# The last sums of a two-block forward pass cut as 384 and 128 tokens, their chunks turned one by one, and the last tile written in two parts

## The chip, the cores and the metric

One core of one Trainium2 chip runs the whole program in one launch. The metric is the device time in microseconds (us). The engines are named as in the profile: PE is TensorE's matmuls, PEld its weight loads, DVE is VectorE, ACT is ScalarE, POOL is GpSimd, and SP is SyncE, which here only issues transfers.

## The reference, cut to what matters

Two transformer blocks follow each other on 16 meta tokens and 512 tokens of width 1024. The part that matters is the very end of the second block: the down projection of its second feed-forward network, the residual sum, and the final norm.

```python
def swiglu_2(x, w_gate, w_up, w_down):
    return (jax.nn.silu(x @ w_gate) * (x @ w_up)) @ w_down      # D_FF = 2816

...
        h = h + 0.5 * swiglu_2(rms_norm(h, ffn2_norm[l]), ...)
    return rms_norm(h, final_norm)                              # out: (1, 512, 1024) f32
```

`rms_norm` divides each token's 1024 values by the root of their mean square and multiplies by a gain for each of the 1024 columns.

## The kernel before

**Layout.** The running sum `h` lies with its 1024 columns over the partitions: eight chunks `h[:, c]` of 128 columns, each with the tokens along the free axis (16 meta tokens, which the output leaves out, then 512). A matmul has 128 x 128 weights and a slice of tokens as its moving operand. Every product is made of three matmuls, since weights and inputs are split into a high and a low part in fp32r: high weights with high input, high weights with low input, low weights with high input (`mm`, L488). Each of the three loads its own weights.

**Weights.** A transfer brings a piece of a weight matrix to one of two raw buffers, ACT casts its high part (`whi`, L120) and DVE subtracts to get the low part (`wlo`, L125). A raw buffer is loaded anew when both have read it.

**The feed-forward network** goes through its 22 chunks of hidden columns in three parts (`PARTS`: 6, 8 and 8). Each part ends with a down projection of what it has, `dn`. In the third part eight chunks of hidden columns (`gh`, `gl`) meet weights for eight output chunks: 24 matmuls for each output chunk and slice of tokens. Four transfers of 1 MB (`in_ffn_w_down`) bring these weights, two output chunks each. `seven` makes the hidden chunks (accumulators `sa`, `sb`, `sc`, L700) and begins the first three `dn` sums with seven of the eight hidden chunks, before the eighth is done: the first sum before the last two products of the eighth (`up_a`, `gate_b`), two more behind them. `up_a` writes the eighth hidden chunk for tokens 16 to 271, `gate_b` for tokens 272 to 527. `finish` adds the eighth.

**The last loop** is where the change lies. It takes the tokens in two halves, `XA = (16, 256)` and `XB = (272, 256)` (start and length), and in each half the eight output chunks `c`:

- PE adds the 24 products in a PSUM bank `dn` (the first three chunks of the first half are those that `seven` began).
- DVE adds the bank to `h` (L1782). ACT squares the sum (L415; L412 for a half's first chunk, L408 for the last half's last), and DVE adds the square to `sqacc` (L416).
- DVE multiplies the sum by the final gain of its columns (`g`, L1786). Two chunks share one tile `g` of 2 x 256.
- After every second chunk `turn_out` is put on a list, and it is run when the next chunk's products have been written: four transposes on PE (`oT<-cst,g`, L1747) turn two chunks for two blocks of 128 tokens, and ACT copies them to the output tiles `o` (L1749), where tokens lie over the partitions.

When a half is summed, `compact` sums the squares over the partitions with matmuls of two columns (`p<-ones,sqacc` and, for the last chunk's square, `p<-ones,sq`, L423) and makes the factor of each token by three Newton steps on DVE (L384 to L391, `nw_v`, `nw_y`). `write` multiplies each tile of 128 tokens by it and sends it out: the first tile of the half by DVE (L1760) and SP's queue, the second by ACT (L1757) and ACT's queue. For the first half this stands behind chunk 1 of the second half; for the second half it is the end of the program.

The order of instructions on each engine is set by a scheduler when the program is built; each engine then works strictly in that order.

Of the kernel before, what the change touches and what calls it, by code (L numbers as in the profile page):

```python
# [8 lines left out]
F32 = mybir.dt.float32  # L9
F32R = mybir.dt.float32r  # L10
I32 = mybir.dt.int32
ACTF = mybir.ActivationFunctionType
ALU = mybir.AluOpType
AX = mybir.AxisListType

P = 128
DM = 1024
KD = 8
DFF = 2816
NM = 16  # L20
# [7 lines left out]
V_F1, V_MIX, V_F2, V_FIN = 48, 56, 64, 72  # L28
# [13 lines left out]

A_SL, B_SL = (0, 272), (272, 256)
XA, XB, XF = (16, 256), (272, 256), (16, 512)


def grid(ap, a):
    return ap.rearrange("p (a b) -> p a b", a=a)
# [175 lines left out]
def two_blocks(ctx: ExitStack, tc, d, out):  # L224
    nc = tc.nc
    pe, act, dve, pool = nc.tensor, nc.scalar, nc.vector, nc.gpsimd

    def open_pool(name, bufs=1, **kw):
        cm = tc.tile_pool(name=name, bufs=bufs, reuse_waits="tile", **kw)
        return cm, cm.__enter__()  # L230

    def close_pool(cm):
        cm.__exit__(None, None, None)
# [9 lines left out]
    def ps(name="ps"):  # L243
        return psp.tile([P, 512], F32, tag="ps", name=name)

    cst = const.tile([P, C_END], F32, name="cst")
    ident = cst[:, C_ID:C_ID + P]
# [8 lines left out]
    accF = hold.tile([P, SEQ], F32, name="accF")  # L256

    def col(i):
        return vec[:, i:i + 1]

    def cut(t, k, sl):
        return t[:, k, sl[0]:sl[0] + sl[1]]
# [131 lines left out]
    sq = {}  # L394

    class Rms:
# [7 lines left out]
        def add(self, src, last=False):  # L404
            n = self.sl[1]
            if self.lone or last:
                t = sq["pool"].tile([P, 272], F32, tag="sqFalse", bufs=sq["bufs"], name="sq")[:, 0:n]
                act.activation(out=t, in_=src, func=ACTF.Square)  # L408
                self.wait.append(t)
            elif self.acc is None:  # L410
                self.acc = accF if n == 512 else sq["pool"].tile([P, 272], F32, tag="sqacc", bufs=2, name="sqacc")[:, 0:n]
                act.activation(out=self.acc, in_=src, func=ACTF.Square)  # L412
            else:
                t = sq["pool"].tile([P, 272 if n <= 272 else 512], F32, tag=f"sq{n > 272}", bufs=sq["bufs"], name="sq")[:, 0:n]
                act.activation(out=t, in_=src, func=ACTF.Square)  # L415
                dve.tensor_tensor(out=self.acc, in0=self.acc, in1=t, op=ALU.add)  # L416
# [65 lines left out]
    def mm(acc, u, kcs, hl, last=None):  # L482

        last = kcs[-1] if last is None else last
        for k in kcs:
            for j, (w, x) in enumerate(((u.hi, hl[0]), (u.hi, hl[1]), (u.lo, hl[0]))):
                for p, sl in acc:
                    pe.matmul(p, lhsT=w[:, k], rhs=cut(x, k, sl), start=(k == 0 and j == 0),  # L488
                              stop=(k == last and j == 2))
# [53 lines left out]
    def run_ffn(ffn, items, slices, down, halves, gcol, xn, spare, last, close_w2=False):  # L543


        cm = None
        if spare is None:
            cm, tp = open_pool("right", side="right")
            W.beside = [tp.tile([P, 512], F32, name=f"rawx{i}") for i in range(2)]
            slots = [Slot(None, *[tp.tile([P, 4 * halves[0][1]], F32R, name=f"x{x}{i}") for x in "hl"])  # L550
                     for i in range(2)]
            w_half, n_half = [(w2, 2)], 2
        else:
            W.beside = [spare[1].tile([P, 512], F32, name=f"rawx{i}") for i in range(2)]
            slots = []
            w_half, n_half = [(w4, 1)], 2
        run_item(items[0], slices)
        slots += [W.reserved.pop(0) for _ in range(3 - len(slots))]
        steps, rest = ffn.prepare(halves, gcol, xn, slots)
        todo, did = items[1:], 0  # L560
        for i, it in enumerate(todo):
            upto = len(steps) * (i + 1) // len(todo)
            run_item(it, slices, steps=steps[did:upto])
            did = upto
        for pool, k in w_half:
            W.reserve(pool, k)
        rest()
        down(0, ())
        for _ in range(n_half):
            W.halve(W.reserved.pop(0))  # L570
        for part in (1, 2):
            first = ffn.seven(range(PARTS[part][1]), slices if part == 1 else last)
            if part == 1:
                down(1, first)
        W.whole(not close_w2)
        own = [x for x in slots if x.pool is not None]
        W.idle.extend(own)
        if cm:
            close_pool(cm)
        return first  # L580
# [374 lines left out]
    p = ps("vt")  # L955
    pe.transpose(p[:, 0:48], gains, ident[0:48, 0:48])
    dve.tensor_copy(out=vec[:, 0:48], in_=p[:, 0:48])
    p = ps("mtT")
# [12 lines left out]
    p = ps("vt")  # L971
    pe.transpose(p[:, 0:P], vrow, ident)
    dve.tensor_copy(out=vec[:, 48:P], in_=p[:, 48:P])
    for i in (1, 5):
        g = vec[:, V_GN[i]:V_GN[i] + KD]
# [12 lines left out]
    i = 0  # L988
    while i < len(order):
        kind, n = order[i]  # L990
# [330 lines left out]
    def add_h(after=None):  # L1321
        def sink(c, sl, p):
            dve.tensor_tensor(out=cut(h, c, sl), in0=p, in1=cut(h, c, sl), op=ALU.add)
            if after:
                after(c)
        return sink
# [389 lines left out]
    for c in ALLK:  # L1716
# [7 lines left out]
    cm_o, op_ = open_pool("outp")  # L1724
    cm_x, wx = open_pool("wx")
# [5 lines left out]
    ob = op_.tile([P, 4, DM], F32, name="o")  # L1731
    sq.update(pool=op_, bufs=2)
    first = run_ffn(ffn, items[2:], ONE, lambda part, first: ffn.down(PARTS[part][1], ONE, add_h(), first), [XA, XB], V_F2,
                    ob.rearrange("p a b -> p (a b)").rearrange("p (k t) -> p k t", k=KD), (wx, op_), [XA])


    halves = [XA, XB]
    fins = {sl: Rms(sl) for sl in halves}
    ot = [ob[:, i] for i in range(4)]

    def turn_out(c, sl, g):

        t0 = (sl[0] - NM) // P
        q = ps("oT")
        for t in range(2):
            for i in range(2):
                pe.transpose(q[:, (2 * t + i) * P:(2 * t + i + 1) * P], g[:, i, t * P:(t + 1) * P], ident)  # L1747
        for t in range(2):
            act.copy(out=ot[t0 + t][:, P * (c - 1):P * (c + 1)], in_=q[:, 2 * t * P:2 * (t + 1) * P])  # L1749

    def write(sl):
        r = fins[sl].r
        t0 = (sl[0] - NM) // P
        for t in range(2):
            o = ot[t0 + t]
            if t:
                act.activation(out=o, in_=o, func=ACTF.Copy, scale=r[:, t:t + 1])  # L1757
                nc.scalar.dma_start(out=out[0, P * (t0 + t):P * (t0 + t + 1)], in_=o)
            else:
                dve.tensor_scalar(out=o, in0=o, scalar1=r[:, t:t + 1], scalar2=None, op0=ALU.mult)  # L1760
                nc.sync.dma_start(out=out[0, P * (t0 + t):P * (t0 + t + 1)], in_=o)

    us, wait = [], []
    ks = list(range(PARTS[2][1]))
    for sl in halves:
        for c in range(KD):
            if first:
                u, (p,) = first.pop(0)
                us.append(u)
                ffn.finish(len(ks), [sl], u, [p])  # L1770
            else:
                if sl == XA:
                    us += W.take(1)
                p = ps("dn")[:, 0:256]
                mm([(p, sl)], us[c], ks, (ffn.gh, ffn.gl))
            if wait:
                wait.pop()()
            if sl == XB and c == 1:
                fins[XA].compact()
                write(XA)  # L1780
            src = cut(h, c, sl)
            dve.tensor_tensor(out=src, in0=p, in1=src, op=ALU.add)  # L1782
            fins[sl].add(src, last=sl == XB and c == KD - 1)
            if c % 2 == 0:
                g = op_.tile([P, 2, 256], F32, tag="g", bufs=2, name="g")
            dve.tensor_scalar(out=g[:, c % 2], in0=src, scalar1=col(V_FIN + c), scalar2=None, op0=ALU.mult)  # L1786
            if c % 2:
                wait.append(lambda c=c, sl=sl, g=g: turn_out(c, sl, g))
    wait.pop()()
    fins[XB].compact()  # L1790
    write(XB)
    close_pool(cm_x)
    close_pool(cm_o)
    ffn.close()
# [44 lines left out]
```

## Time and profile before

| | us |
|---|---|
| median of 3 runs | 2034.89 (2034.45 to 2038.19) |
| profiled execution, its own time | 2036.98 |
| its span, first to last instruction | 2035.2 |
| PE busy | 1995.0 (98%) |
| DVE busy | 1486.4 (73%) |
| ACT busy | 1063.4 (52%) |
| mean granted TensorE clock | 0.994 |

The profiled execution's own time is 1.8 us more than its span, and 2.1 us more than the median. The trace's times count from the first instruction of the span. A matmul's row gives its start and a modelled length; matmuls overlap, so the pace of PE is read from the distance between starts.

### The profile page before, as it was taken

How to read it: one execution, taken by the hardware profiler on the slowest of the kernel's cores; microseconds unless marked ns; L12 is line 12 of the kernel's file. 1: busy time of each engine (PE TensorE's matmuls, PEld its weight loads, DVE VectorE, ACT ScalarE, POOL GpSimd, SP SyncE). 2: the span in 40 equal slices, each digit the busy share in tenths (PEclk: the TensorE clock that was granted, in tenths of full speed). 3: DMA queues.
4: the chain of work that ended last, by engine and by line, in shares of the span. 5: the costliest groups of instructions: out<-in, count | busy, mean ns of one | idle time of the engine just before them, and what ended most of it. 6: DMA issues, size and time to landing. Idle time of an engine off the chain costs nothing.

```text
span 2035.2 us, 34893 instructions
## 1 busy us (share of the span) xinstructions
PE 1995.0 (98%) x13583; PEld 1833.5 (90%) x13583; DVE 1486.4 (73%) x2949; ACT 1063.4 (52%) x2030; POOL 283.2 (14%) x290
## 2 busy tenths in 40 slices
PE   8999999999999999999999999999999999999998
PEld 8999999989989989899998998987777788898998
DVE  5948578777776767668777775876889868685784
ACT  5445345357765445445443543656878743353552
POOL 0012021023420002111000211103211100120210
PEclk9999999999999999999999999999999999999999
DMA  6357575237784238566532766737545353475761
GB/s 182 93 116 166 131 149 147 84 81 174 149 147 125 73 93 166 146 139 157 151 78 78 162 149 140 156 116 159 102 98 114 76 152 99 108 162 140 147 163 44
DMA packets 413212, 260.10 MB, mean 128 GB/s; under 512 B 17483, under 2 KB 405830, under 8 KB 413046
## 3 DMA queue, kind: packets, MB, share of 16 engines
q1 hardware_dynamic: 317446, 192.94, 32.1%
q0 software_dynamic: 95040, 63.69, 22.1%
q8 instruction: 106, 1.74, 0.3%
q10 hardware_dynamic: 560, 1.24, 0.2%
q14 instruction: 60, 0.49, 0.1%
HBM read 230.53 MB, written 4.23 MB: 115 GB/s over the span
## 4 chain that ended last, share of the span: by engine, by line
PE 84%; DVE 8%; ACT 4%; DMA 2%; issue 1%; POOL 0%; ACTq 0%; POOLq 0%; DVEq 0%; SPq 0%
PE dn L488 25%; PE sa L700 18%; PE acc L488 14%; PE sc L700 8%; PE sb L700 4%; PE accB L488 3%; PE accA L488 3%; PE wo L488 2%; DVE wlo L125 1%; ACT whi L120 1%; PE ro L1611 1%; PE p L423 1%; PE num L1202 1%; PE ms L1469 1%; DMA raw<-in_w_uq 1%
## 5 line engine op out<-in xcount | busy, mean ns | idle before, releaser
L120 ACT CAST whi<-raw 128x1024 fp32r<-128x1024 f32 (+3 forms) x500 | 397.5, 801 | 346.3 <-PE dn L488 168.5
L125 DVE TENSOR_TENSOR wlo<-raw,whi 128x512 fp32r<-128x512 f32 (+2 forms) x456 | 406.2, 905 | 134.7 <-ACT whi L120 130.6
L488 PE MATMUL dn<-gh,whi 128*128 128x256 f32 (+2 forms) x908 | 277.5, 326 | 0.6 <-ACT gh L469 0.6
L488 PE MATMUL dn<-gl,whi 128*128 128x256 f32 (+2 forms) x908 | 277.9, 326 | 0.0
L488 PE MATMUL dn<-gh,wlo 128*128 128x256 f32 (+2 forms) x908 | 277.0, 325 | 0.0
L488 PE MATMUL acc<-nh,whi 128*128 128x512 f32 (+2 forms) x600 | 191.0, 353 | 1.1 <-DVE y L1219 1.1
L488 PE MATMUL acc<-nl,whi 128*128 128x512 f32 (+2 forms) x600 | 188.5, 349 | 0.0
L488 PE MATMUL acc<-nh,wlo 128*128 128x512 f32 (+2 forms) x600 | 188.1, 348 | 0.0
L488 PEld LDWEIGHTS dn<-gh,whi 128*128 128x128 f32 x908 | 163.0, 188 | 16.5 <-ACT gh L469 0.8
L488 PEld LDWEIGHTS dn<-gl,whi 128*128 128x128 f32 x908 | 163.1, 188 | 15.5 <-DVE gl L470 0.3
L488 PEld LDWEIGHTS dn<-gh,wlo 128*128 128x128 f32 x908 | 163.2, 188 | 14.8
L700 PE MATMUL sc<-nh,whi 128*128 128x256 f32 (+1 forms) x488 | 137.4, 282 | 0.0
L700 PE MATMUL sa<-nh,whi 128*128 128x256 f32 (+1 forms) x488 | 137.3, 281 | 0.0
L700 PE MATMUL sa<-nh,wlo 128*128 128x256 f32 (+1 forms) x488 | 137.2, 281 | 0.0
L700 PE MATMUL sc<-nh,wlo 128*128 128x256 f32 (+1 forms) x488 | 137.2, 281 | 0.0
L700 PE MATMUL sc<-nl,whi 128*128 128x256 f32 (+1 forms) x488 | 137.1, 281 | 0.0
L700 PE MATMUL sa<-nl,whi 128*128 128x256 f32 (+1 forms) x488 | 137.0, 281 | 0.0
L488 PEld LDWEIGHTS acc<-nh,whi 128*128 128x128 f32 (+1 forms) x600 | 104.6, 188 | 16.4 <-DVE y L1219 1.6
L488 PEld LDWEIGHTS acc<-nh,wlo 128*128 128x128 f32 (+1 forms) x600 | 104.0, 188 | 15.0
L488 PEld LDWEIGHTS acc<-nl,whi 128*128 128x128 f32 (+1 forms) x600 | 103.9, 188 | 13.6
L95 POOL DMA_DIRECT2D raw<-in_ffn_w_up x32 | 41.1, 1284 | 448.8 <-DMA raw<-in_ffn_w_up 229.1
L95 POOL DMA_DIRECT2D raw<-in_ffn_w_in x32 | 41.1, 1283 | 439.4 <-DMA raw<-in_ffn_w_in 163.6
(494 smaller groups left out, 5583.1 us busy)
## 6 DMA issues: line engine op xcount, KB each, us to landing
raw<-in_ffn_w_in SPq DMA_DIRECT2D x56, 512.0 KB, 4.1
raw<-in_ffn_w_gate SPq DMA_DIRECT2D x44, 512.0 KB, 3.6
raw<-in_ffn_w_in SPq DMA_DIRECT2D x64, 256.0 KB, 3.2
raw<-in_ffn_w_out SPq DMA_DIRECT2D x16, 1024.0 KB, 8.0
wlo<-raw POOLq DMA_DIRECT2D x32, 512.0 KB, 5.3
raw<-in_ffn_w_up SPq DMA_DIRECT2D x64, 256.0 KB, 3.2
raw<-in_ffn_w_down SPq DMA_DIRECT2D x16, 1024.0 KB, 7.4
raw<-in_a_w_in SPq DMA_DIRECT2D x18, 512.0 KB, 3.6
```

Source lines behind the costliest of these rows:

```text
L95: self.nc.gpsimd.dma_start(out=dst(t), in_=src, accum_op=ALU.add)
L120: nc.scalar.copy(out=ho, in_=src)
L125: self.lo_engine.tensor_tensor(out=lw, in0=src, in1=ho.bitcast(F32), op=ALU.subtract)
L423: pe.matmul(self.p1[:, self.n:self.n + 2], lhsT=src[:, o:o + P], rhs=ones[:, 0:2], start=True, stop=True)
L488: pe.matmul(p, lhsT=w[:, k], rhs=cut(x, k, sl), start=(k == 0 and j == 0), stop=(k == last and j == 2))
L700: pe.matmul(acc, lhsT=w[:, 4 * i + k], rhs=x[:, k], start=start and k == 0 and j == 0, stop=k == 3 and j == 2, skip_group_check=not start)
L1202: pe.matmul(num[:, c0:SEQ], lhsT=w[0:kk, j], rhs=x[s_], start=(j == 0 and i == 0), stop=(j == 4 and i == 2))
L1469: pe.matmul(s, lhsT=mq[i][a][:, t0:t0 + P], rhs=mk[i][b], start=j == 0, stop=j == 2)
L1611: pe.matmul(o[i], lhsT=vt_[:, i, j], rhs=s_[i, j][b], start=(j == 0 and b == 0), stop=(j == 3 and b == 1))
```

## The change

The two slices of tokens of the last loop become `FA = (16, 384)` and `FB = (400, 128)`: three blocks of 128 tokens, then one. Each chunk has a tile `g` of its own and is turned by itself, so a `turn_out` has three transposes in the first slice and one in the second, and one ACT copy. The sum of squares of the long slice lies in `accF`, and its squares after the first chunk are made and added in two pieces of 192. `write` goes over three tiles (DVE, ACT, DVE) for the first slice, and for the last tile over two pieces of 512 columns: the first by DVE and SP's queue, the second by ACT and ACT's queue.

```diff
+FA, FB = (16, 384), (400, 128)
...
-                self.acc = accF if n == 512 else sq["pool"].tile([P, 272], F32, tag="sqacc", bufs=2, name="sqacc")[:, 0:n]
+                self.acc = accF[:, 0:n] if n > 272 else sq["pool"].tile([P, 272], F32, tag="sqacc", bufs=2, name="sqacc")[:, 0:n]
                 act.activation(out=self.acc, in_=src, func=ACTF.Square)
+            elif 272 < n < 512:
+                for c in (slice(0, n // 2), slice(n // 2, n)):
+                    t = sq["pool"].tile([P, 272], F32, tag="sqFalse", bufs=sq["bufs"], name="sq")[:, 0:n // 2]
+                    act.activation(out=t, in_=src[:, c], func=ACTF.Square)
+                    dve.tensor_tensor(out=self.acc[:, c], in0=self.acc[:, c], in1=t, op=ALU.add)
...
-                    ob.rearrange("p a b -> p (a b)").rearrange("p (k t) -> p k t", k=KD), (wx, op_), [XA])
+                    ob.rearrange("p a b -> p (a b)").rearrange("p (k t) -> p k t", k=KD), (wx, op_), [FA])
...
-    halves = [XA, XB]
+    halves = [FA, FB]
...
-        t0 = (sl[0] - NM) // P
-        q = ps("oT")
-        for t in range(2):
-            for i in range(2):
-                pe.transpose(q[:, (2 * t + i) * P:(2 * t + i + 1) * P], g[:, i, t * P:(t + 1) * P], ident)
-        for t in range(2):
-            act.copy(out=ot[t0 + t][:, P * (c - 1):P * (c + 1)], in_=q[:, 2 * t * P:2 * (t + 1) * P])
+        t0, n = (sl[0] - NM) // P, sl[1] // P
+        q = ps("oT")[:, 0:sl[1]]
+        for t in range(n):
+            pe.transpose(q[:, t * P:(t + 1) * P], g[:, t * P:(t + 1) * P], ident)
+        act.copy(out=ob[:, t0:t0 + n, P * c:P * (c + 1)], in_=grid(q, n))
...
-        for t in range(2):
+        for t in range(sl[1] // P):
             o = ot[t0 + t]
...
+            row = out[0, P * (t0 + t):P * (t0 + t + 1)]
+            for i in range(2 if sl == FB else 1):
+                c = slice(512 * i, 512 * i + 512) if sl == FB else slice(0, DM)
+                if (t + i) % 2 == 0:
+                    dve.tensor_scalar(out=o[:, c], in0=o[:, c], scalar1=r[:, t:t + 1], scalar2=None, op0=ALU.mult)
+                    nc.sync.dma_start(out=row[:, c], in_=o[:, c])
+                else:
+                    act.activation(out=o[:, c], in_=o[:, c], func=ACTF.Copy, scale=r[:, t:t + 1])
+                    nc.scalar.dma_start(out=row[:, c], in_=o[:, c])
...
-            if c % 2 == 0:
-                g = op_.tile([P, 2, 256], F32, tag="g", bufs=2, name="g")
-            dve.tensor_scalar(out=g[:, c % 2], in0=src, scalar1=col(V_FIN + c), scalar2=None, op0=ALU.mult)
-            if c % 2:
-                wait.append(lambda c=c, sl=sl, g=g: turn_out(c, sl, g))
+            g = op_.tile([P, 384], F32, tag="g", bufs=2, name="g")[:, 0:sl[1]]
+            dve.tensor_scalar(out=g, in0=src, scalar1=col(V_FIN + c), scalar2=None, op0=ALU.mult)
+            wait.append(lambda c=c, sl=sl, g=g: turn_out(c, sl, g))
```

In the changed file the lines below the edit stand 6 or 7 further down (L1782 is L1789, L488 is L494). All engines keep their order up to the first `dn` of the last part on PE, and up to the last weights on DVE and ACT.

The first place is DVE's queue where the last loop begins. `wlo_...` are the low parts of the last down projection's weights; `raw_86` holds the fourth and last transfer in the rows of `wlo_17930` and `wlo_17932`, which before stand further down. Before the change the queue reads:

```order
L125 TENSOR_TENSOR wlo_17928<-raw_85,whi_17927 128x1024
L724 SCALAR_TENSOR_TENSOR sqFalse<-sqacc,sqFalse 128x256
L1782 TENSOR_TENSOR h<-dn,h 128x256
L470 TENSOR_TENSOR gl<-sqFalse,gh 128x256
L1786 TENSOR_SCALAR g<-h,vec 128x256
L1782 TENSOR_TENSOR h<-dn,h 128x256 x2
```

The same place of DVE's queue in the changed kernel reads:

```order
L730 SCALAR_TENSOR_TENSOR sqFalse<-sqacc,sqFalse 128x256
L476 TENSOR_TENSOR gl<-sqFalse,gh 128x256
L126 TENSOR_TENSOR wlo_17930<-raw_86,whi_17929 128x1024
L126 TENSOR_TENSOR wlo_17932<-raw_86,whi_17931 128x1024
L1789 TENSOR_TENSOR h<-dn,h 128x384 x2
L1792 TENSOR_SCALAR g<-h,vec 128x384 x2
```

The first sums `h` stood ahead of the last weights' low parts and now stand behind both of them; ACT's two casts `whi_17929` and `whi_17931` likewise stand ahead of the first square now.

The second place is the end of PE's queue: the last `dn` matmuls, the last transposes, and the sums of squares. Before the change it reads:

```order
L488 MATMUL dn<-gh,whi_17931 128x256
L488 MATMUL dn<-gl,whi_17931 128x256
L488 MATMUL dn<-gh,wlo_17932 128x256
L1747 MATMUL oT<-cst,g 128x128
L423 MATMUL p_21529<-ones,sqacc 128x2 x2
L1747 MATMUL oT<-cst,g 128x128 x3
L423 MATMUL p_21529<-ones,sq 128x2 x2
```

The end of PE's queue in the changed kernel reads:

```order
L494 MATMUL dn<-gh,whi_17931 128x128
L494 MATMUL dn<-gl,whi_17931 128x128
L494 MATMUL dn<-gh,wlo_17932 128x128
L1752 MATMUL oT<-cst,g 128x128 x2
L429 MATMUL p_21568<-ones,sqacc 128x2
L429 MATMUL p_21568<-ones,sq 128x2
```

The matmuls are as many as before, 24 for each chunk, with 128 columns for 256; behind the last of them two transposes stand instead of four, and two sums of squares instead of four.

## Rows read from the trace of the kernel before

**Rows 1.** Page, part 1: busy time of each engine.
```profile
PE 1995.0 (98%) x13583; PEld 1833.5 (90%) x13583; DVE 1486.4 (73%) x2949; ACT 1063.4 (52%) x2030; POOL 283.2 (14%) x290
```

**Rows 2.** Chain that ended last, from 1984 us on (start, length, what).
```profile
1991.22 0.44 PE oT L1747 x4
1991.65 5.68 PE dn L488 x48
...
2006.68 0.34 PE p L423 x4
...
2025.41 0.44 DVE h L1782
...
2027.21 0.17 DVE nw_v L439
...
2029.39 1.15 ACT o L1757
```

**Rows 3.** PE's timeline: first and last `dn` of the last part, its wait.
```profile
1972.79 0.28 PE L488 MATMUL dn<-gh,whiwide 128*128 128x256 f32 x1
...
1984.88 0.33 PE L1747 MATMUL oT<-cst,g 128*128 128x128 f32 x1 [0.60 <-DVE g L1786]
...
2025.10 0.28 PE L488 MATMUL dn<-gh,wlo 128*128 128x256 f32 x1
2025.22 0.27 PE L1747 MATMUL oT<-cst,g 128*128 128x128 f32 x1
```

**Rows 4.** PE's timeline: runs of 400 columns and of 144, first and last.
```profile
471.76 0.35 PE L1202 MATMUL num<-sl,vh 128*128 128x400 f32 x1
...
472.31 0.34 PE L1205 MATMUL den<-sl,onesr 128*128 128x400 f32 x1
...
479.38 0.27 PE L1202 MATMUL num<-sl,vh 128*128 128x144 f32 x1
...
479.72 0.27 PE L1205 MATMUL den<-sl,onesr 128*128 128x144 f32 x1
```

**Rows 5.** Timelines of SP, ACT and DVE where the last loop begins.
```profile
1980.32 0.37 SPq L99 DMA_DIRECT2D raw<-in_ffn_w_down  x1
...
1983.70 0.41 ACT L469 CAST gh<-sqFalse 128x256 fp32r<-128x256 f32 x1 [1.85 <-DVE sqFalse L724]
...
1985.58 1.03 ACT L120 CAST whi<-raw 128x1024 fp32r<-128x1024 f32 x1
...
1984.14 0.42 DVE L470 TENSOR_TENSOR gl<-sqFalse,gh 128x256 fp32r<-128x256 f32 x1
...
1984.75 0.74 DVE L1782 TENSOR_TENSOR h<-dn,h 128x256 f32<-128x256 f32 x2
...
1986.64 1.23 DVE L125 TENSOR_TENSOR wlo<-raw,whi 128x1024 fp32r<-128x1024 f32 x1 [0.25 <-ACT whi L120]
```

**Rows 6.** Page, part 6: transfers of these weights, median us from issue to landing.
```profile
raw<-in_ffn_w_down SPq DMA_DIRECT2D x16, 1024.0 KB, 7.4
```

**Rows 7.** Groups by line and shape on DVE: busy us, mean ns.
```profile
L1782 DVE TENSOR_TENSOR h<-dn,h 128x256 f32<-128x256 f32 x16 | 6.7, 423 | 15.7 <-PE dn L488 15.7
L1786 DVE TENSOR_SCALAR g<-h,vec 128x256 f32<-128x256 f32 x16 | 5.6, 352 | 0.4
L1760 DVE TENSOR_SCALAR o<-o,nw_y 128x1024 f32<-128x1024 f32 x2 | 1.5, 755 | 0.1
L454 DVE TENSOR_SCALAR dg<-cst,nw_y 128x128 f32<-128x128 f32 x44 | 10.7, 293 | 4.3 <-PE p L455 3.7
L1481 DVE TENSOR_SCALAR mp<-mp,su 128x512 f32<-128x512 f32 x16 | 7.7, 483 | 0.3
```

**Rows 8.** End of the program: last issues, and transfers in 40 slices from 2030 to 2036 us.
```profile
2030.18 0.36 SPq L1761 DMA_DIRECT2D out<-o  x1
...
2030.57 0.37 ACTq L1758 DMA_DIRECT2D out<-o  x1
...
GB/s 0 0 0 0 0 0 55 382 410 437 410 410 437 410 410 355 410 437 382 437 355 355 437 410 55 0 0 55 0 0 0 0 0 0 0 0 0 0 0 0
```

**Rows 9.** Windows, by engine busy us (x instructions), then granted clock, DMA.
```profile
411.20:414.60 3.40, 3.06 (x29) 2.77 (x28) 1.91 (x10) 2.08 (x6) 0.00 (x0) 1.00 0.00 0
414.60:421.40 6.80, 6.78 (x32) 6.73 (x33) 4.73 (x19) 1.61 (x3) 0.00 (x0) 0.50 0.11 25
670.00:676.40 6.40, 6.40 (x58) 6.34 (x57) 2.08 (x13) 2.50 (x6) 0.00 (x0) 1.00 0.01 3
```

More of the change, by code (lines that the diff above doesn't have):

```diff
@@ L1753, in write @@
         t0 = (sl[0] - NM) // P
-        for t in range(2):
+        for t in range(sl[1] // P):
             o = ot[t0 + t]
[L1756 to L1761, printed above, removed]
+            row = out[0, P * (t0 + t):P * (t0 + t + 1)]
[7 more added lines that the diff above has]
+                    nc.scalar.dma_start(out=row[:, c], in_=o[:, c])
     us, wait = [], []
@@ L1771, in two_blocks @@
             else:
-                if sl == XA:
+                if sl == FA:
                     us += W.take(1)
-                p = ps("dn")[:, 0:256]
+                p = ps("dn")[:, 0:sl[1]]
                 mm([(p, sl)], us[c], ks, (ffn.gh, ffn.gl))
@@ L1777, in two_blocks @@
                 wait.pop()()
-            if sl == XB and c == 1:
-                fins[XA].compact()
-                write(XA)
+            if sl == FB and c == 1:
+                fins[FA].compact()
+                write(FA)
             src = cut(h, c, sl)
             dve.tensor_tensor(out=src, in0=p, in1=src, op=ALU.add)
-            fins[sl].add(src, last=sl == XB and c == KD - 1)
-            if c % 2 == 0:
-                g = op_.tile([P, 2, 256], F32, tag="g", bufs=2, name="g")
-            dve.tensor_scalar(out=g[:, c % 2], in0=src, scalar1=col(V_FIN + c), scalar2=None, op0=ALU.mult)
-            if c % 2:
-                wait.append(lambda c=c, sl=sl, g=g: turn_out(c, sl, g))
+            fins[sl].add(src, last=sl == FB and c == KD - 1)
+            g = op_.tile([P, 384], F32, tag="g", bufs=2, name="g")[:, 0:sl[1]]
+            dve.tensor_scalar(out=g, in0=src, scalar1=col(V_FIN + c), scalar2=None, op0=ALU.mult)
+            wait.append(lambda c=c, sl=sl, g=g: turn_out(c, sl, g))
     wait.pop()()
-    fins[XB].compact()
-    write(XB)
+    fins[FB].compact()
+    write(FB)
     close_pool(cm_x)
```

## Prediction

> **What bounds the kernel now.** I read the page's busy times first: PE is busy for 1995.0 of 2035.2 us [rows 1], so what lengthens PE's stream lengthens the kernel, unless the end gets shorter. The chain that ended last agrees for the part that changes: from 1984 us to 2025 us it is `dn` matmuls and transposes on PE, in runs such as 48 `dn` in 5.68 us and four `oT` in 0.44 us, and only behind the last `dn` does it leave PE, for DVE, ACT and the last transfers [rows 2]. PE's timeline shows one wait there, 0.60 us for a `g` from DVE at 1984.88 us [rows 3]. So the change has three places: PE's stream from the first `dn` at 1972.79 us to the last one at 2025.10 us, the wait at its head, and the tail behind 2025.38 us, where the last `dn` ends (start and length of its row) [rows 3].
>
> **PE's stream.** The last part has 8 x 24 = 192 matmuls for each of the two slices, before and after. What changes is their width, so I need the pace of 384 and of 128 columns. At 256 the chain has 48 in 5.68 us, which is 0.118 us each [rows 2]. Wider: between the first and the last row of the run of 400 columns lie three steps in 0.55 us, 0.183 each [rows 4]. On the line through 256 and 400 (0.00045 us a column) 384 columns take 0.176. Narrower: in the run of 144 columns three steps take 0.34 us, 0.113 each [rows 4]; four transposes of 128 columns take 0.44, 0.110 each, and four sums of two columns stand in the chain with 0.34 [rows 2]. So below some 245 columns a matmul with weights of its own gets no faster: its pace is that of loading 128 x 128 weights. The 128-token slice will pay about 0.112 for each matmul, hardly less than 0.118 for twice the tokens.
>
> The sum: before 384 x 0.118 = 45.3 us. After 192 x 0.176 = 33.8 and 192 x 0.112 = 21.5, together 55.3. That is +10.0 us. Bounds: the narrow pace from 0.110 to 0.118 gives -0.4 to +1.2 around it, the wide one 0.172 to 0.179 gives -0.8 to +0.6.
>
> The row shows 0.113 at 144 columns [rows 4]. The Trainium skill's page "TensorE: Matmul & The Clock Gate", in its section on the back-to-back issue gap, puts the steady pace of pairs of a weight load and a 128-column matmul at about 81 ns. By that the narrow slice would take 192 x 0.081 = 15.6 us, an estimate from that page, the stream would grow by 4.1 and not by 10.0, and the whole sum below would end near 2037.7. The trace does not agree with it for these 4-byte operands, so I go by the row.
>
> Transposes: 28 of the 32 stood ahead of the last `dn`'s end or beside it, now 30 do. At 0.11 each that is +0.2. The first slice's factors need three sums of two columns for four, -0.1. More interruptions with fewer transposes in each cost nothing by themselves, since each pays by its weight loads. The 16 + 8 squares in pieces, the gains and the copies lie on ACT and DVE beside PE: before, DVE waited 15.7 us for PE in front of the 16 `h` [rows 7], and in the long slice a chunk now gives it 4.2 us of PE's time for about 1.8 us of its own work. If that cover were gone, banks would fill and PE would wait for `h`; nothing points to it. The two tiles that DVE now scales for the first slice (2 x 0.755 [rows 7]) stand ahead of the third narrow chunk's `h` and `g`; PE has two chunks of 2.7 us to do meanwhile, some 5 us, against about 4.5 for Newton's steps and the two tiles. That is hidden with little to spare.
>
> **The wait at the head.** PE will come to the first transpose later: from 1972.79, 21 x 0.176 + 24 x 0.118 (the eighth hidden chunk's products, still 256 wide) + 51 x 0.176 = 15.5 us, so at 1988.3. But DVE's first `h` now stands behind the low parts of the last weights. Their transfer was issued at 1980.32, and ACT cast from it at 1985.58, when its squares were done [rows 5]; so it had landed by then, and I take 1985.0. Then: one cast of 1.05, two low parts at some 1.15 each (1.23 less the overlap) [rows 5], so 1988.4; two `h` of 384 at about 0.5, two `g` at about 0.4 (scaled by width from [rows 7]), so 1990.1; transposes of the first chunk run under the second's `g`, and three more at 0.11 follow. The next `dn` starts at about 1990.45. Without a wait it would be 1988.3 + 6 x 0.11 = 1988.96. So the wait is 1.5 us for 0.60: +0.9. Bounds: no wait at all (-0.6), or landing at 1985.58 (+1.5). The other new need, that the first `finish` also wants `gate_b`'s half of `gl`, costs nothing: that is DVE's row at 1984.14 [rows 5], and PE comes there at 1986.7.
>
> **The tail.** Before: from the last `dn`'s end at 2025.38 to the end of the span 9.8 us. Behind it came `h` (0.42), the `g` of the pair's second half, three transposes and four sums, and `nw_v` began at 2027.21, 1.83 us later [rows 2]. After: `h` and `g` of 128 tokens take about 0.29 each (the 128-wide row has 0.293 [rows 7]) instead of 0.423 and 0.352, and one transpose and two sums follow `g`: 0.03 + 0.29 + 0.04 + 0.29 + 0.04 + 0.33 for the starts and some 0.13 of the last sum's length, about 1.15. That is -0.7. Newton's steps stay: their time is that of a fixed number of small instructions. Scaling: DVE's 512 columns take 0.483 for 0.755 [rows 7], so SP issues 0.27 earlier. It is SP's issue that counts: before, SP issued at 2030.18 and ACT at 2030.57, and the two transfers of 512 KB moved without a gap from about 2030.9 to 2033.7 at some 400 GB/s [rows 8], so ACT's 1.15 us of scaling [rows 2] was not last. Half as many bytes take 1.4 us less. Together -0.7 - 0.27 - 1.4 = -2.3. Bounds: if rows of 2 KB move no faster by the piece, only -1.0; if all three come out better, -2.8.
>
> **The sum.** +10.0 + 0.1 + 0.9 - 2.3 = +8.7 us. The profiled execution took 2036.98, so it would be 2045.7; it stood 2.1 above the median of the runs shown, so against that median of 2034.89 I predict **2043.6**.
>
> **Rivals.**
>
> *Narrow matmuls go at the pace of their columns.* Then 128 columns take 0.118 - 128 x 0.00045 = 0.060, the slice costs 11.5 for 21.5, and the sum is 10.0 less: -1.3, so 2033.6, not slower. It decides from a pace below 0.112 - 8.7/192 = 0.067. For it: nothing but the line through the wide shapes. Against it: 144, 128 and two columns all stand at 0.11 [rows 2, 4]. A pace in between (about 0.08) would give 2037.5.
>
> *The clock falls in the narrow stage.* TensorE's granted clock fell from 1.00 to 0.50 (2.4 to 1.2 GHz) at 414.6 us, and in the 3.4 us ahead PE had been busy for 3.06 with narrow and half-filled work; 32 matmuls then took 6.8 us, 0.21 each [rows 9]. If the narrow slice were paced so, it would cost up to 192 x 0.10 = 19 more: up to 2062.8, or 2053 if it falls halfway. Against it: from 670.0 to 676.4 us, 58 matmuls, more than half of them sums of two columns with full weights, kept 1.00 [rows 9].
>
> *The last weights land late.* If the fourth transfer takes the median 7.4 us [rows 6] from its issue, it lands at 1987.7, and DVE's `h` and so PE wait 2.7 us longer: 2046.3. Against it: ACT had them at 1985.58 before, and the changed DVE order frees the buffer no later.
>
> *The end gains nothing from smaller pieces*, because a small transfer is all latency: -1.0 for -2.3, which is 2044.9. The steady 400 GB/s [rows 8] speaks against it.
>
> **How the numbers follow.** What a measurement of this kernel can tell from no change is about 0.2%, 4 us. I give my forecast 0.80 (here the fourth rival lies in its bounds), the late landing 0.05, the falling clock 0.07, the pace by columns 0.05 and the one between 0.03. The bounds of the terms (-0.4 to +1.2, -0.8 to +0.6, -1.5 to +0.6 for the wait, -0.5 to +1.3 for the tail) hardly all fall on one side; with some 1 us for the measurement they give 2040.5 to 2046.5, and up to 2047.5 the late landing is in as well. Slower by over 0.2% (above 2039.0) are the forecast less a small part, the late landing and the falling clock: 0.89. Within 0.2%: both cases of cheap narrow matmuls and a little of the forecast, 0.08. Faster: 0.03.
>
> **What would show it.** Right: in the last 21 us or so of `dn` 24 matmuls of 128 columns take 2.7 us, and in the long slice 4.2; PE waits once, about 1.5 us, for `g` behind the last `wlo`; from the last `dn`'s end to the end of the span it is about 7.5 us; the granted clock stays at 1.00 until the last `dn`. Wrong: 24 narrow matmuls in 1.5 us (then the kernel is no slower), or in 5 us with a granted clock of 0.50; a second wait for `g` behind the two tiles that DVE scales; or a tail of over 8.8 us.

## The result, and the profile after

The changed kernel takes 2048.19 us in the median of six runs (2043.55 to 2051.0), the kernel before 2036.6 beside it (2034.45 to 2038.19): a ratio of 1.0055, 95% interval 1.0044 to 1.0066. It is slower, as forecast, but by 11.6 us and not by 8.7, and the median lies 0.7 us above the range's end of 2047.5.

The profiled run has a span of 2046.35 us for 2035.21. Split as the prediction does:

| us | before | after | difference | predicted |
|---|---|---|---|---|
| start of the span to the first `dn` of the last part | 1972.79 | 1974.87 | +2.1 | 0 |
| first `dn` to the last one's end | 52.59 | 63.49 | +10.9 | +11.0 |
| the last `dn`'s end to the end of the span | 9.83 | 8.00 | -1.8 | -2.3 |

Below, the second row is called the stage, the third the tail, and PE's wait in front of the first transposes the head wait. The page's part 1, which answers to [rows 1], has PE busy for 11.9 us more:

```profile
PE 2006.9 (98%) x13581; PEld 1843.9 (90%) x13581; DVE 1488.2 (73%) x2957; ACT 1064.4 (52%) x2037; POOL 283.1 (14%) x290
```

The chain that ended last in the changed kernel, from the last weights' transfer on (start, length, what), answers to [rows 2]:

```profile
1981.82 5.34 DMA raw<-in_ffn_w_down
...
1987.19 1.06 ACT whi L121
...
1988.27 2.36 DVE wlo L126 x2
1990.63 0.93 DVE h L1789 x2
1991.56 0.34 DVE g L1792
...
1991.94 0.88 PE oT L1752 x6
1992.82 4.19 PE dn L494 x24
...
2015.47 2.63 PE dn L494 x24
...
2021.22 0.56 PE p L429 x6
...
2038.39 0.30 DVE h L1789
...
2039.06 0.33 PE oT L1752
2039.39 0.36 PE p L429 x4
...
2039.77 0.17 DVE nw_v L445
...
2041.89 0.72 ACT o L1767
```

24 `dn` of 384 columns take 4.19 us, 0.175 each, and 24 of 128 columns 2.63, 0.110 each, where 48 of 256 took 5.68 [rows 2], 0.118 each. A third of the tokens at the long slice's rate would take 4.19/3 = 1.40; the narrow slice takes 1.23 more for each of the eight chunks, 9.8 together, which is nearly all that the stage lost. The head of the chain is no longer PE but the transfer of the last weights, ACT's cast, DVE's two low parts and `h`: PE waits for them, as PE's timeline shows in the brackets, the answer to [rows 3]:

```profile
1974.87 0.33 PE L494 MATMUL dn<-gh,whiwide 128*128 128x384 f32 x1
...
1991.94 0.88 PE L1752 MATMUL oT<-cst,g 128*128 128x128 f32 x6 [1.41 <-DVE g L1792]
...
2038.08 0.28 PE L494 MATMUL dn<-gh,wlo 128*128 128x128 f32 x1
2038.19 0.30 PE L1752 MATMUL oT<-cst,g 128*128 128x128 f32 x1
2039.06 0.33 PE L1752 MATMUL oT<-cst,g 128*128 128x128 f32 x1 [0.57 <-DVE g L1792]
```

Adding each matmul's distance to the next start over the whole stage, without the waits, the `dn` take 34.3 + 21.6 = 55.8 us for 46.1 before (+9.8), the transposes and the sums of two columns +0.3, and the wait +0.8.

Windows of the changed kernel (long slice, narrow slice, tail) show the granted clock at 1.00 wherever PE's stream is the bound. The columns are those of [rows 9]: window, its length, busy time (x instructions) of PE, PEld, DVE, ACT and POOL, granted clock, DMA share, GB/s.

```profile
1992.82:2010.91 18.09, 18.09 (x109) 17.95 (x109) 6.52 (x17) 4.10 (x13) 0.00 (x0) 1.00 0.00 1
...
2024.65:2038.19 13.54, 13.54 (x125) 13.54 (x124) 4.91 (x16) 3.09 (x11) 0.00 (x0) 1.00 0.30 117
2038.36:2046.35 7.99, 0.80 (x6) 0.58 (x5) 2.79 (x15) 1.55 (x4) 0.00 (x0) 0.72 0.18 67
```

DVE's two whole tiles of the first slice stand in its timeline as one row, and no PE wait follows them:

```profile
2023.88 1.42 DVE L1764 TENSOR_SCALAR o<-o,nw_y 128x1024 f32<-128x1024 f32 x2
2025.21 0.28 DVE L1789 TENSOR_TENSOR h<-dn,h 128x128 f32<-128x128 f32 x1
```

The end of the program, which answers to [rows 8]: the last issues, and the last transfers in 40 slices from 2041 to 2047 us.

```profile
2042.40 0.33 SPq L1765 DMA_DIRECT2D out<-o  x1
...
2042.65 0.37 ACTq L1768 DMA_DIRECT2D out<-o  x1
...
GB/s 0 0 0 0 0 0 0 0 0 0 0 0 0 0 82 287 410 396 396 396 341 396 382 341 69 55 0 0 0 0 0 0 0 0 0 0 0 0 0 0
```

The packets of the two transfers reach from 2043.23 to 2044.83 us, 1.60 us for 512 KB; before, they reached from 2031.04 to 2033.80, 2.76 us for 1 MB. So half the bytes take 1.2 us less, not 1.4.

### The profile page after: what moved, and what is told of

The parts are those of the page before. It is cut to its first block, busy times and chain, and to the rows that moved or that the text cites. A ratio compares the mean times of both kernels' runs of the same rounds, so it can differ in the third digit from the quotient of the medians.

```text
span 2046.4 us, 34907 instructions
## 1 busy us (share of the span) xinstructions
PE 2006.9 (98%) x13581; PEld 1843.9 (90%) x13581; DVE 1488.2 (73%) x2957; ACT 1064.4 (52%) x2037; POOL 283.1 (14%) x290
## 4 chain that ended last, share of the span: by engine, by line
PE 79%; DVE 9%; ACT 5%; DMA 3%; issue 3%; POOL 1%; ACTq 0%; POOLq 0%; DVEq 0%; SPq 0%
PE dn L494 24%; PE sa L706 17%; PE acc L494 12%; PE sc L706 8%; PE sb L706 4%; PE accB L494 3%; PE accA L494 3%; PE wo L494 2%; DVE wlo L126 1%; ACT whi L121 1%; DMA raw<-in_ffn_w_down 1%; PE p L429 1%; PE ro L1617 1%; DMA raw<-in_w_uq 1%; DMA raw<-in_ffn_w_out 1%
## 5 line engine op out<-in xcount | busy, mean ns | idle before, releaser
L494 PE MATMUL dn<-gh,whi 128*128 128x512 f32 (+4 forms) x908 | 280.5, 330 | 0.9 <-ACT gh L475 0.7
L494 PE MATMUL dn<-gl,whi 128*128 128x512 f32 (+4 forms) x908 | 280.9, 330 | 0.0
L494 PE MATMUL dn<-gh,wlo 128*128 128x512 f32 (+4 forms) x908 | 279.9, 329 | 0.0
L494 PE MATMUL acc<-nh,whi 128*128 128x512 f32 (+2 forms) x600 | 191.2, 353 | 1.1 <-DVE y L1225 1.1
L494 PE MATMUL acc<-nl,whi 128*128 128x512 f32 (+2 forms) x600 | 188.5, 349 | 0.0
L494 PE MATMUL acc<-nh,wlo 128*128 128x512 f32 (+2 forms) x600 | 188.2, 348 | 0.0
L494 PEld LDWEIGHTS dn<-gh,whi 128*128 128x128 f32 x908 | 163.3, 188 | 17.0 <-ACT gh L475 1.5
L494 PEld LDWEIGHTS dn<-gl,whi 128*128 128x128 f32 x908 | 163.2, 188 | 15.5 <-DVE gl L476 0.3
L494 PEld LDWEIGHTS dn<-gh,wlo 128*128 128x128 f32 x908 | 163.4, 189 | 14.8
L494 PEld LDWEIGHTS acc<-nh,whi 128*128 128x128 f32 (+1 forms) x600 | 104.6, 188 | 16.5 <-DVE y L1225 1.6
L494 PEld LDWEIGHTS acc<-nh,wlo 128*128 128x128 f32 (+1 forms) x600 | 104.1, 188 | 15.1
L494 PEld LDWEIGHTS acc<-nl,whi 128*128 128x128 f32 (+1 forms) x600 | 103.9, 188 | 13.6
```

## The experiments

The theory is the prediction's sum: the narrow slice pays for weight loads and not for columns, the head pays for low parts that moved ahead of `h`, and the tail gives back 2 us. Eight kernels ran, in two groups of four on two chips, each timed against the kernel before (2036.04 us in the median of 23 runs in the first group, 2035.71 of 23 in the second).

**Both kernels once more, unchanged.**

> The kernel before, unchanged, as a kernel of its own: it shows how far two equal programs lie apart, and where. Call D the time from the start of the first dn matmul of the last part to the end of the last one, and T from there to the end of the span; before D was 52.6 and T 9.8 us, with the first dn at 1972.8. If only the last part matters: ratio within 0.1% of 1, D 52.3 to 52.9, T 9.6 to 10.0, and the first dn anywhere between 1971 and 1975, since that is scatter of parts that the change leaves alone. If the start of the last part is fixed by the program: first dn at 1972.8 within 0.5 us.

> The changed kernel once more. Theory: the change costs D 63.5 (10.9 more) and T 8.0 (1.8 less), together 9.1 us, and the 2.1 us by which the last part began later (1974.9) was scatter, part of it a fall of the clock at 1611.8 us in a stage that is the same in both. Then D and T repeat within 0.4, the first dn lies at 1971 to 1975 with no fall of the clock at 1612 or one in the kernel before too, and the ratio is 1.0040 to 1.0050. Rival: the changed program is slower ahead of the last part too, always: first dn at 1974.5 or later again, the clock low at 1612 again, ratio 1.0055 or more.

The kernel before: ratio 1.0005 (0.9993 to 1.0017), median 2036.34 of 12 runs that reach from 2030.31 to 2044.25. The changed kernel: 1.0047 (1.0035 to 1.0059), median 2044.11 of 5 (2043.12 to 2048.35). The stage takes 52.90 and 63.21 us here, the tail 9.85 and 8.06, the head wait 0.87 and 1.07: differences of +10.3 and -1.8, +8.5 together, for +9.1 in the first pair. The first `dn` stands at 1975.03 and 1975.31, so the 2.1 us that the first pair showed ahead of the change are not there.

**Columns or weight loads?** The short slice's matmuls go over 256 columns, of which the last 128 are used; the rest is as in the changed kernel.

```diff
-                p = ps("dn")[:, 0:sl[1]]
-                mm([(p, sl)], us[c], ks, (ffn.gh, ffn.gl))
+                if sl == FB:
+                    p = ps("dn")[:, 0:256]
+                    mm([(p, XB)], us[c], ks, (ffn.gh, ffn.gl))
+                    p = p[:, 128:256]
```

> The changed kernel, with the 192 matmuls of the short slice made 256 columns wide (tokens 272 to 527), of which the last 128 are used: twice the columns for the same result. If the pace of the narrow ones is that of loading their weights: 0.118 for 0.110 each, D 1.6 more than in the changed kernel (65.1), T 8.0, ratio to the kernel before 1.005. If columns set the pace: 0.058 more each, D 11 more (74.6), ratio 1.010.

Ratio 1.0054 (1.0041 to 1.0066), median 2046.72. Two chunks of the short slice in this kernel's chain:

```profile
2016.31 2.81 PE dn L494 x24
...
2028.96 2.83 PE dn L494 x24
```

Twice the columns cost 0.2 us a chunk, 1.7 us for the 192 matmuls by their starts (23.25 for 21.58). If columns set the pace, the kernel with 128 would have had to be 11 us faster than this one. The stage is 65.73 us, 2.2 more: these 1.7, a head wait of 2.13 for 1.41, for weights that landed later, and 0.2 less for the transposes. So 128 columns run at a floor, and the rival of a pace by columns is out. The changed kernel's chain puts this floor at 2.63/24 = 0.110 us. The Trainium skill's page "TensorE: Matmul & The Clock Gate" has a rule that comes near it in another section than the one weighed in the prediction: under "LDWEIGHTS (loading the stationary operand)" a load takes as many nanoseconds as it has columns, divided by 1.2, which is 107 for 128. The trace agrees with that one, and not with the 81 ns of the issue gap.

**What the single turns and the two parts do alone.** Two kernels keep the halves of 256 and take the rest of the change: one with the last two tiles in two parts each, one with all tiles written whole. Against the changed kernel the first is

```diff
-FA, FB = (16, 384), (400, 128)
+FA, FB = XA, XB
```

and the second adds

```diff
-            for i in range(2 if sl == FB else 1):
-                c = slice(512 * i, 512 * i + 512) if sl == FB else slice(0, DM)
+            for i in range(1):
+                c = slice(0, DM)
```

> The changed kernel with the slices of the kernel before (256 and 256 tokens): chunks turned singly, and both tiles of the last half scaled and written in two parts each. Theory: PE's stream is as before, D 52.6 within 0.5; in the tail two transposes instead of three stand behind the last g, SP issues 0.27 earlier and the same bytes move, so T is 9.3 to 9.5, and the ratio 0.999 to 1.000. Rival: small transfers cost more than they bring, T 9.8 to 10.5.

> The kernel before with single turns alone: halves of 256, tiles written whole. If single turns by themselves cost only what the earlier run with two-part tiles showed at the head and behind the last products, the stage takes 53.3 to 53.8 us for 52.6 to 52.9, from the last dn to the first of Newton's steps 2.2 us for 1.83, the tail 10.2 us, and the kernel is about 1 us longer, which is hardly told from 1.000. If that run's extra came from the parts alone, the stage stays at 52.6 to 52.9 and the tail at 9.8. First dn from 1972 to 1975 us.

With parts: ratio 1.001 (1.0001 to 1.0019), stage 53.68, tail 10.51. Whole: 1.0009 (0.9997 to 1.002), stage 53.22, tail 10.17. So with halves nothing of the rest makes the tail shorter, and my 9.3 to 9.5 for the first was a miss. The stages are longer than before's 52.6 and 52.9 because PE waits twice at the head, 0.47 and 0.48 us whole and 0.81 and 0.49 with parts, and because the `dn` take 0.3 to 0.5 us more by their starts when more turns stand between them. Single turns lengthen the tail by 0.3 us; where that comes from shows at the end of PE's timeline with tiles written whole:

```profile
2024.31 0.38 PE L1752 MATMUL oT<-cst,g 128*128 128x128 f32 x2
2025.37 0.44 PE L1752 MATMUL oT<-cst,g 128*128 128x128 f32 x2 [0.69 <-DVE g L1792]
2025.65 0.51 PE L429 MATMUL p<-ones,sqacc 128*128 128x2 f32 x4
2026.02 0.59 PE L429 MATMUL p<-ones,sq 128*128 128x2 f32 x4
```

Before, the sums over `sqacc` stood behind the first of the last transposes, that is, in PE's wait for `g`; now they stand behind the last transpose, and the first of Newton's steps comes 2.17 us behind the last `dn` for 1.83. With parts the rest behind Newton's last step takes 6.25 us for 5.92. The timelines of ACT and SP:

```profile
2030.04 1.33 ACT L1767 ACTIVATE o<-o,nw_y 128x512 f32<-128x512 f32 x2 [2.59 <-DVE nw_y L390]
2030.79 0.95 ACTq L1768 DMA_DIRECT2D out<-o  x2
...
2030.54 0.83 SPq L1765 DMA_DIRECT2D out<-o  x2
```

Each engine now scales and issues twice, and the last issue ends at 2031.74, 1.80 us behind Newton's end, for 1.65 before (2030.57 + 0.37 [rows 8], against 2029.29). That is a small loss and no gain. Counted from Newton's end, the last packets of the output end at 4.86 us, and at 4.50 in the kernel before, its repeat and the one with tiles written whole, so the 0.33 goes with the parts in this profile. A rest of one profile can scatter as much, though: the kernel before with moved low parts (below) has 6.26 with whole tiles.

**Does the last tile in two parts bring anything?** The same edit of the loop in the changed kernel, which has one tile left to write at the end.

> The changed kernel, but the last tile is scaled whole by DVE and written whole by SP's queue. By the prediction's sum two parts bring DVE 0.27 us and the bytes nothing, so the tail would be 8.0 + 0.3 = 8.3 us. The rival: a transfer of 256 KB in rows of 2 KB took 0.83 and 0.93 us in the changed kernel's profile, one of 512 KB in rows of 4 KB 1.44, so one whole transfer is as quick as two parts or quicker, and the tail is 7.9 to 8.1 us. Everything ahead of the tail is as in the changed kernel (63.2 to 63.5 us). First dn at 1974.8 to 1975.4 us if the changed program is slower ahead of the last part, from 1972 on if that is scatter.

Ratio 1.0049 (1.003 to 1.0068), median 2044.85. The tail is 8.35 us for 8.00 and 8.06, all of it behind Newton's last step (4.91 for 4.55 and 4.61). DVE's scaling and SP's issue in this kernel:

```profile
2038.07 0.75 DVE L1764 TENSOR_SCALAR o<-o,nw_y 128x1024 f32<-128x1024 f32 x1
...
2038.85 0.33 SPq L1765 DMA_DIRECT2D out<-o  x1
```

The issue comes 0.78 us behind the scaling's start, for 0.56 with a half tile; the packets take 1.55 us for 1.60. Counted from Newton's end, the issue comes at 0.89 us for 0.60, and the last packets of the output end at 3.27 for 3.03. So the parts bring some 0.3 us in this profile, 0.22 of it through DVE's shorter scaling and the bytes nothing: the prediction's 0.27, and not the rival.

**Is the head wait DVE's low parts?** In both kernels the low parts of the last two weights go to ACT and an accumulating transfer of POOL's queue. The edit also moves two low parts of the first block, which ACT now makes between 352 and 358 us, so the stage says more here than the ratio.

```diff
-                if self.lo_engine is None:
+                if self.lo_engine is None or self.n_split >= len(self.subs) - 2:
```

> The changed kernel, but the low parts of the last two weights are no longer made by DVE: the same work goes to ACT and to an accumulating transfer of POOL's queue, as elsewhere in the program. If the head wait (1.41 us at 1991.94 us in the changed kernel's profile) comes from h standing behind those two low parts on DVE, it shrinks to 0 to 0.3 us, and the stage from the first dn to the last one's end takes 62.1 to 62.5 us for 63.5; the tail stays at 8.0. If the wait is for the transposes' input in any case, because PE comes there early, it stays above 1 us and the stage at 63.2 or more. A third way: the accumulating transfer lands late, and PE waits instead for the low parts ahead of the last chunks' products; then a new wait for POOL's queue shows there. Ratio to the kernel before 1.0040 to 1.0050. On the question whether the changed program is slower ahead of the last part as well: the first dn stood at 1972.0 to 1975.0 us in three profiles of programs with halves, and at 1974.9 to 1975.3 in three with 384 and 128; if the difference is of the program, it stands at 1974.8 to 1975.4 here too, if it is scatter, it may stand anywhere from 1972 to 1975.4.

> The kernel before, with the low parts of the last two weights moved off DVE as in the other run. The head wait there (0.60 and 0.87 us in two profiles) stands behind h and g, which already stand ahead of those low parts, so it should stay at 0.3 to 0.9 us, and the stage at 52.2 to 52.9 us, the tail at 9.8. If the low parts cost that wait too, it vanishes and the stage takes 52.0. Either way the ratio is 0.999 to 1.001. First dn from 1972 to 1975 us.

Changed kernel: ratio 1.0042 (1.0028 to 1.0057), stage 62.86. PE's wait, and DVE's `h` ahead of it, which now waits for PE:

```profile
1990.39 1.19 PE L1752 MATMUL oT<-cst,g 128*128 128x128 f32 x6 [0.47 <-DVE g L1792]
...
1988.91 1.09 DVE L1789 TENSOR_TENSOR h<-dn,h 128x384 f32<-128x384 f32 x2 [2.78 <-PE dn L494]
1989.91 1.07 DVE L1792 TENSOR_SCALAR g<-h,vec 128x384 f32<-128x384 f32 x2
```

The wait is 0.47 us, for 1.41, 1.07 and, in the kernel with one part, 1.79. So 0.6 to 1.3 us of it were the low parts; the 0.47 that stay are DVE's own two `h` ahead of the first `g`, which neither of my two cases held. The stage gains less, 0.3 to 1.1 us against the 63.21, 63.49 and 63.91 of the three kernels, since the six transposes now take 1.19 us for 0.88.

With the low parts on DVE, the wait follows the start of ACT's cast of the last weights. Here are that cast and the wait in the repeat of the changed kernel, in the kernel with one part and in the one with 256 columns:

```profile
1987.31 1.99 ACT L122 CAST whi<-raw 128x1024 fp32r<-128x1024 f32 x2
1992.06 0.88 PE L1753 MATMUL oT<-cst,g 128*128 128x128 f32 x6 [1.07 <-DVE g L1793]
...
1983.30 2.00 ACT L121 CAST whi<-raw 128x1024 fp32r<-128x1024 f32 x2 [1.15 <-DMA raw<-in_ffn_w_down]
1988.06 0.88 PE L1752 MATMUL oT<-cst,g 128*128 128x128 f32 x6 [1.79 <-DVE g L1792]
...
1987.98 2.00 ACT L121 CAST whi<-raw 128x1024 fp32r<-128x1024 f32 x2 [1.40 <-DMA raw<-in_ffn_w_down]
1992.74 0.88 PE L1752 MATMUL oT<-cst,g 128*128 128x128 f32 x6 [2.13 <-DVE g L1797]
```

Counted from the first `dn` the cast starts at 12.0, 12.7 and 13.0 us, and at 12.3 in the changed kernel's first profile; in each of the four the wait is that time less 10.9.

The kernel before, so changed: ratio 1.0012 (1.0003 to 1.0021), head wait 0.57, close to its earlier 0.60 and 0.87: there the low parts were not in the way. Instead PE now waits for the transfer, which brings the stage to 53.32 us, outside what I expected; so is the tail, 10.17, whose cause was not followed. In this kernel's waits of PE:

```profile
PE oT L1747 <- DVE g L1786: 1.0, 2, 0.6
PE dn L488 <- DMA wlo<-raw: 0.5, 1, 0.5
```

This is the third way of the expectation, though in the other kernel. No run points to a version faster than both kernels: the kernel before stands within 0.2% of every one with halves, and ahead in the median.

## Why the prediction was right, and where it was not

**PE's stream: right.** +10.0 predicted, +9.8 by the matmuls' starts; 24 narrow ones in 2.63 us (2.7 predicted) and 24 wide ones in 4.19 (4.2). The run with 256 columns shows the floor directly. The sums on both sides were too small, 46.1 and 55.8 measured for 45.3 and 55.3: turns between the `dn` cost something, 0.4 us for single turns alone, where the prediction had nothing, and the paces it took were high by 0.7 us in all, so it is in part luck that the difference comes out. One reading did not show what it was taken for: four sums of two columns in 0.34 us are 0.085 each and not 0.11; the first of the four starts 0.03 us ahead of the second, and the others stand 0.11 apart.

**The head: right.** +0.9 predicted; +0.8 in the first pair, +0.2 in the second, as ACT's cast of the last weights falls. The path was as described: both low parts, two `h`, `g`, transposes. From the first `dn`, the weights were there after 12.3 us (ACT's cast at 1987.19) for the 12.2 of the sum, `h` began after 15.8 (1990.63 in the chain) for 15.6, and the next `dn` after 17.95 for 17.7. The run without them shows that 0.6 to 1.3 us of the wait come from them.

**The tail: right in kind, 0.5 too large.** -2.3 predicted, -1.8 measured twice. To `nw_v` it is 1.42 us for 1.15: `h` and `g` took their 0.29, but from the last transpose's start to the end of the sums it is 0.69 (2039.06 to 2039.75) for the 0.46 that I had. In the trace each sum is two rows (the four `p` behind the last transpose are the order's two), and the length of the last is 0.36 for my 0.13. The bytes gave 1.2 for 1.4. The 0.27 of the shorter scaling was right.

**The step that failed** is in the paragraph on how the numbers follow: "with some 1 us for the measurement", put on a base of three runs. The sum of +8.7 measured +9.1 and +8.5, so the terms did not carry the median out of the range. The profiled run of the changed kernel, 2048.15 us, is nearly the median run, and it shows where its 4.6 us over the forecast lie: 2.1 in the later first `dn`, 0.4 in the terms, and 2.1 that the forecast took off because the profile before stood that much above the median of its three runs. Of the 2.1 ahead of the first `dn`, 1.1 is a fall of the clock (last section). Up to that `dn` PE, DVE, ACT and POOL have the same order of instructions in eight of the ten profiles; the two with moved low parts differ in the two of the first block. It stands at

| | us |
|---|---|
| halves (five profiles) | 1971.25, 1972.01, 1972.79, 1975.03, 1975.62 |
| 384 and 128 (five profiles) | 1970.61, 1974.26, 1974.87, 1974.94, 1975.31 |

Both lists reach over 4 us and overlap, with means of 1973.5 and 1974.0, so a cause in the changed program is not needed for this, and a shift of a us or two can't be excluded by them. The later medians speak against a large one: the repeat, the kernel with 256 columns and the one with one part stand 8.1, 10.7 and 9.1 us above the kernel before, 0.5 to 0.8 less than their profiles' stages and tails give over the first profile's 62.4. The kernel with moved low parts stands 9.6 above, 1.1 more than its profile gives. The same kernel's runs scatter more: 2043.12 to 2051.0 for the changed one in two groups, 2030.31 to 2044.25 in one for the kernel before. Against this I made two choices too narrow: I took the median of three runs of before as the base, 2034.89, where later groups of 23 have 2035.7 and 2036.0, and I allowed 1 us for the rest. With 2036.0 as the base the sum gives 2044.7; the six runs' median lies 3.5 above that, the repeat's 0.6 below. That the six stood high by scatter is what these numbers suggest; it isn't shown run by run, as a trace exists for one run of each kernel only.

Of the rivals, the pace by columns is out by the run with 256; the falling clock did not come (1.00 to 2038.19); ACT's cast of the last weights began 12.0 to 13.0 us behind the first `dn`, for the sum's 12.2 and the rival's 14.9, so the late landing came by 0.8 us at most. That small pieces gain nothing at the end is in part so: the bytes came to 0.2 less than thought, and the gain to Newton's step to 0.3 less.

## What to carry to other kernels

A slice narrower than the width at which PE's step meets its weight load saves hardly any PE time (1.7 us of 23 here for half the columns), so cutting 256 + 256 as 384 + 128 cost PE 9.8 us of 46: look for that width in two rows of different shapes before moving a boundary to shorten a tail. Splitting the last output over two engines and queues paid only while the second was idle: in one profile each, 0.3 us gained with one tile left, none with two. And a range needs the scatter of the program's untouched stretches, not only the bounds of the changed one: 5 us here, for a change of 9.

## What the runs showed of the hardware that was not expected

Part of the scatter ahead of the change is the granted clock, which fell at one place of the program in four of ten profiles and not in the others. Around 1611 us in the changed kernel it reads as in the first two windows below (columns as in [rows 9]), at the same place in the kernel before as in the third and fourth:

```profile
1605.00:1611.80 6.80, 4.30 (x27) 3.21 (x26) 6.20 (x13) 6.69 (x13) 0.99 (x1) 1.00 0.01 1
1611.80:1615.21 3.41, 3.40 (x10) 2.51 (x9) 3.35 (x6) 1.86 (x4) 0.56 (x1) 0.50 0.87 108
```

```profile
1603.79:1610.59 6.80, 4.31 (x27) 3.21 (x26) 6.21 (x13) 6.69 (x13) 0.99 (x1) 1.00 0.01 1
1610.59:1614.00 3.41, 3.30 (x16) 2.58 (x15) 3.35 (x6) 1.86 (x4) 0.56 (x1) 1.00 0.87 108
```

PE did the same in the 6.80 us ahead, 27 matmuls and 4.30 or 4.31 us busy; then the clock stays at 1.00 (2.4 GHz) in the kernel before, and is at 0.50 (1.2 GHz) for 3.41 us in the changed one, where 10 matmuls ran in the time of 16. By the same instructions' starts on DVE, each of the four profiles with the fall loses 1.1 to 1.3 us there against the kernel before, and none of the others more than 0.1. What decides between the two is open. By the same starts most of the other differences arise between 150 and 425 us and between 1200 and 1600 us; they were not followed further.
